# A hybrid encoder step on one core: a planner that lays out every instruction gets new rules for DMA issue, landing and stores

## The chip, the cores and the metric

The kernel runs on one core of one Trainium2 chip. The metric is device microseconds (us) of one execution; less is better. Three timed executions of the kernel before give a median of 1089.2 us (1089.12 to 1092.17).

## The reference

One inference step of an encoder layer, for 512 prompt tokens and 64 later tokens that are handled together (576 columns), in float32:

```python
x = x + mixer(rmsnorm(x))        # gated DeltaNet branch and gated linear attention branch, merged by gates, then w_o
x = x + cross_attn(rmsnorm(x), mem)   # 4 heads of 256 into 256 memory tokens: w_mk, w_mv, w_mq, w_mo
x = x + conv_ffn(rmsnorm(x))     # w_up (1024 -> 2*2816), causal depthwise conv, SiLU gate, w_down
y = rmsnorm(x)                   # and the new states, conv rows and memory keys/values as outputs
```

The model width is 1024, so `x` is eight tiles `x[0]` to `x[7]` of 128 features by 576 tokens. Nearly all work is matrix products of weights by those tiles.

## The kernel before

**Precision.** Each float32 product is made of float32r products: a weight tile is loaded raw (`wr`, 128 x 1024 float32, 512 KB), split into a high part `h` and a low part `lo` (both called `w`), and high x high, high x low and low x high are added in PSUM (`sm`). The split of most weights is "summed": ScalarE writes minus raw into `lo` and the rounded raw into `h`, and a second DMA from GpSimd's queue adds the weight from DRAM onto `lo` (`split_summed`, `accumulate`). The rest are split by a ScalarE copy and a subtraction on VectorE or GpSimd (`X`).

**Seven products for eight.** Many weights go in pairs of tiles through a scheme with seven half-size products, `P1`, `P2`, `P3`, `Q4` to `Q7`, in the order that `product_order` gives. `P1`, `P2` and `Q4` use a quarter of the raw weight pair, the others sums of quarters (`ws`, made on VectorE or GpSimd). In `products` each product is 4 x 3 matmuls; three banks hold the results (`a` for P1, Q6, Q7, Q4; `b` for Q5 and P3; `c` for P2), and `finish` adds a bank to the residual, after which the next product may write on it. For `w_o` this is `wo_finish`, a VectorE operation on `x[m]` or `x[m + 1]`, for the pairs of `WPAIRS` (0,1), (2,3), (4,5), (6,7).

**Stages around the change.** `ATT` sets the order after the mixer: memory keys and values (`mem_keys` with tile `kraw` and the store to `o_mk`; `mem_values` with `vraw` and `o_mv`), heads mk0, mv0, mv1, mk1, mk2, then the four `wo` pairs, then mv2, mk3, and the queries. The residual `x` is loaded a second time for `wo`, by `x_again`: all eight tiles at the first memory value (`("mv", 0)`). The last big stage is the FFN: `ffn_order` lays out the 22 up tiles (`upx` products from tile 4 on) and puts pieces of the down projection (`dn1`) behind up tiles by the table `AFTER`; what is left of them comes after the last up tile.

**What sets the order.** A planner, `Driver`, runs when the program is built. It keeps a clock `now` that follows TensorE, and a list of busy intervals for VectorE (`V`), ScalarE (`A`), GpSimd (`G`) and the transfer of the DMA rings (`D`). Every operation is placed in the first gap (`place`) that is not before its inputs and not more than `BACK` (6 us) before `now`; `put` hands its start to a heap, and `flush` emits the heap in order of those starts. So the planned times decide nothing but the order in which each engine's queue, and SyncE's DMA queue (SP), holds its instructions. On the chip each queue runs in that order and waits with semaphores. Raw weights live in five buffers (`RAWB` 4 and `RF` 1 in the later stages), split weights in nine (`WB` 6 and `WF` 3); `fetch` emits the loads of coming weights as soon as nine are enough for what is already split.

```python
def load(self, out, in_):
    cost = self.FIXED["D"] + free(out) * self.PACE["D"]          # 0.01 + columns * 0.0016
    start = self.place("D", max(self.ready_at(out), self.latest(self.seen, out)) + 2.2, cost)
    self.mark(self.wrote, start + cost, [out])
    self.put(start - 2.2, [(self.sync.dma_start, (out, in_), {})])
def store(self, out, in_, issuer=None):
    cost = self.FIXED["D"] + free(in_) * self.PACE["D"]
    start = self.place("D", self.ready_at(in_) + 2.2, cost)
    self.mark(self.seen, start + cost, [in_])
    self.put(start - 2.2, [((issuer or self.sync).dma_start, (out, in_), {})])
```

Of the kernel before, what the change touches and what calls it, by code (L numbers as in the profile page):

```python
# [14 lines left out]
ALU = mybir.AluOpType  # L15
# [3 lines left out]
D = 1024  # L19
# [18 lines left out]
HOP = 0.2  # L38
BACK = 6.0
MARGIN = 0.3  # L40
NWARM = 11


# [56 lines left out]
def product_order(pairs, late=False):  # L100

    seq = []
    for i, pair in enumerate(pairs):
        now = [(pair, p) for p in (("P1", "P2", "Q5", "Q6", "P3", "Q7") if late and i == 0 else
                                   ("P1", "Q5", "Q6", "P3", "Q7", "P2", "Q4") if i == len(pairs) - 1 else
                                   ("P1", "Q5", "Q6", "P2", "P3", "Q7"))]
        if i:
            now.insert(2, (pairs[i - 1], "Q4"))  # L110
        seq += now
    return seq
# [10 lines left out]
ATT = [("mk", 0), ("mv", 0), ("mv", 1), ("mk", 1), ("mk", 2), ("wo", 0), ("mv", 2), ("mk", 3), ("mq", 0), ("mq", 1), ("mq", 2), ("mq", 3), ("mv", 3)]  # L123
MPAIRS = [(("mo", m), ("mo", m + 1)) for m in range(2, 8, 2)]
JS = 4
AFTER = {7: 2, 8: 2, 9: 2, 10: 2, 13: 2, 14: 2, 15: 2, 16: 2, 20: 2, 21: 2}


def up_pair(j):
# [3 lines left out]
def ffn_order():  # L133

    seq, old = [("up", j) for j in range(JS)], []
    for j in range(JS, NJ):
# [3 lines left out]
        for i, q in ((j, "P1"), (j - 1, "Q7"), (j, "Q5"), (j, "P2"), (j - 1, "Q4"), (j, "Q6"), (j, "P3")):  # L140
            if i >= JS:
                seq.append(("upx", (i, q)))
        n = AFTER.get(j, 0)
        seq, old = seq + old[:n], old[n:]
# [36 lines left out]
def free(ap):  # L181
    n = 1
    for d in ap.shape[1:]:
        n *= d
    return n


class Engine:


    def __init__(self, drv, key, eng):
        self.drv, self.key, self.eng = drv, key, eng
# [4 lines left out]
    def weigh(self, calls):  # L197
        cost, aps, outs = 0.0, [], []
        for name, args, kw in calls:
# [5 lines left out]
            else:  # L205
                twice = self.key == "V" and len(ins) == 1 and self.port([(name, args, kw)])
                cost += self.drv.FIXED[self.key] + n * self.drv.PACE[self.key] * (0.5 if twice else 1.0)
            cost += 0.06 * (name == "scalar_tensor_tensor" or self.key == "V" and a[0].shape[-1] <= 128 and any(v.space == bass.MemoryType.PSUM for v in a[1:]))
# [41 lines left out]
class Driver:  # L250
# [1 line left out]

    FIXED = dict(V=0.15, A=0.17, G=0.2, D=0.01)
    PACE = dict(V=1 / 960, A=1 / 1180, G=1 / 465, D=512 / 320e3)

    def __init__(self, pe, sync):
        self.pe, self.sync = pe, sync
        self.chains = []  # L260
        self.done = set()
        self.now = 0.0
        self.half = self.type = None
        self.last = 0.0
        self.swapped = 0.0
        self.wrote = {}
        self.seen = {}
        self.ringed = {}
        self.busy = dict(V=[], A=[], G=[], D=[], port=[])
        self.ring = {}  # L270
        self.pending, self.fresh = set(), set()
        self.heap = []
        self.count = 0
        self.waiting = []
# [98 lines left out]
    def note(self, key, cost, outs, aps, fns, port=False):  # L373
# [4 lines left out]
        self.last = max(self.last, end)  # L378
        self.put(start, fns)

    def load(self, out, in_):
        cost = self.FIXED["D"] + free(out) * self.PACE["D"]
        start = self.place("D", max(self.ready_at(out), self.latest(self.seen, out)) + 2.2, cost)
        self.mark(self.wrote, start + cost, [out])
        self.put(start - 2.2, [(self.sync.dma_start, (out, in_), {})])

    def store(self, out, in_, issuer=None):
        cost = self.FIXED["D"] + free(in_) * self.PACE["D"]
        start = self.place("D", self.ready_at(in_) + 2.2, cost)
        self.mark(self.seen, start + cost, [in_])  # L390
        self.put(start - 2.2, [((issuer or self.sync).dma_start, (out, in_), {})])

    def accumulate(self, out, in_, issuer):

        issue = self.place("G", self.open([out], []), 1.0)
        cost = self.FIXED["D"] + 2 * free(out) * self.PACE["D"]
        end = self.place("D", issue + 2.0, cost) + cost + 1.0
        self.mark(self.wrote, end, [out])
        self.put(issue, [(issuer.dma_start, (out, in_), dict(accum_op=ALU.add))])

    def hold(self, fn, cost, args, kw):
        out, ins = args[0], args[1:]
# [38 lines left out]
    def advance(self, c):  # L441
        self.last = self.now
        r = next(c[1])
        if r is None:
            c[0] = self.last + MARGIN
        elif isinstance(r, list):
            c[0] = self.ready_at(*r) + MARGIN
        elif r != WAIT:
# [53 lines left out]
def tile_trunk(ctx, tc, xT, memT, wt, wd, vec, cst, w0, wgate, st_gdn, st_conv, st_gla, st_ffn, ckT, cv,  # L502
# [3 lines left out]
    V, A, G = Engine(drv, "V", nc.vector), Engine(drv, "A", nc.scalar), Engine(drv, "G", nc.gpsimd)  # L506
# [15 lines left out]
    def nm(s):  # L522
        cnt[0] += 1
        return f"{s}{cnt[0]}"

    def slot(s="s", dt=F32, w=SLOT):
        return drv.rotate("s", NS, sp.tile([P, w], dt, tag="s", name=nm(s)))
# [33 lines left out]
    def r4(ap, b=128):  # L561
        return ap.rearrange("p (a b) -> p a b", b=b)
# [180 lines left out]
    pw = pq.tile([P, 512], F32, tag="sm", name=nm("warm"))  # L743
    for _ in range(NWARM):
        PE.matmul(pw, ones_r, ones_r.unsqueeze(1).broadcast_to([P, 4, 128]), start=True, stop=True)
# [13 lines left out]
    for k in range(KT):  # L759
# [3 lines left out]
        if k in WPART:  # L763
            i, a, b = WPART[k]
# [136 lines left out]
    def use_norm(key):  # L901
        N["rt"], N["rbc"] = N[key]

    def xs_of(hl, w=T):
        return [(a[:, 0:w], b[:, 0:w]) for a, b in hl]
# [82 lines left out]
    def evac(ps, dst):  # L988
        for i, r, o in pieces(ps, N["rbc"], dst):
            V.tensor_tensor(o, i, r, op=ALU.mult)  # L990
# [691 lines left out]
    def xslot(i, s="x"):  # L1682

        return drv.rotate(f"F{i}", 1, fp.tile([P, SLOT], F32R if s != "x" else F32, tag=f"F{i}", name=nm(s), bufs=1))


    def main():
# [52 lines left out]
        for k in range(KT + 1):  # L1740
            for i, ps in enumerate(first2):
                j = k - i
# [210 lines left out]
        def x_again(m):  # L1953

            for i in (m, m + 1):
                x[i] = xslot(i)
                DMA(x[i][:, 0:T], xT[:, i, :])
# [4 lines left out]
        out = []  # L1962

        def wo_finish(pair, prod, a, b, c):
            m = pair[0][1]
            xx, scale = (x[m], 0.5) if prod in ("P1", "Q6", "P3", "P2") else (x[m + 1], -0.5)
            half = N1 if prod in ("P1", "P2", "Q4") else N2
            V.scalar_tensor_tensor(xx[:, half], b if prod in ("Q5", "P3") else c if prod == "P2" else a, scale, xx[:, half],
                                   op0=ALU.mult, op1=ALU.add)
            if prod == ("P2" if m == 6 else "P3"):  # L1970
                drv.spawn(c_norm(m, C_GMEM, acc, out))
            elif prod == "Q4":
                drv.spawn(c_norm(m + 1, C_GMEM, acc, out))

        def c_norm(m, gcol, acc_, out_):
            yield [x[m]]
            sq_acc(acc_, x[m], m == 0)
            drv.done.add(("sq", m))
            if drv.ready(*(("sq", i) for i in range(8))):
                drv.spawn(c_rstat("n2", [(acc_, 0)], 4, True, 2.0))  # L1980
            while not drv.ready("wo"):
                yield WAIT
            out_.append((m, norm_prep(x[m], vcol(gcol + m))))
            drv.done.add(("norm", gcol, m))

        for kd, i in ATT:
            if kd == "mk":
                yield from mem_keys(i)
            elif kd == "mv":
                if i == 0:  # L1990
                    for j in range(0, 8, 2):
                        x_again(j)
                yield from mem_values(i)
            elif kd == "wo":
                yield tuple(("wop1", m) for m in range(1, 8, 2))
                yield from products(WPAIRS, [wops[m] for m in range(1, 8, 2)], wo_finish, tuple(("wops", m) for m in range(1, 8, 2)))
                drv.done.add("wo")
            else:
                if i == 0:
                    yield tuple(("norm", C_GMEM, m) for m in range(8))  # L2000
                    xs = xs_of([p for _, p in sorted(out, key=lambda t: t[0])])
                ckr, cvr = slot("ckr"), slot("cvr")
                DMA(r4(ckr[:, 0:512], 256), ckT[:, 2 * i:2 * i + 2, :])
                DMA(r4(cvr[:, 0:512], 256), cv[:, 256 * i:256 * i + 256].rearrange("(a p) d -> p a d", p=P))
                N["ks", i], N["vs", i] = split(ckr), cvr
                for m in (2 * i, 2 * i + 1):
                    b = []
                    yield from tile_proj("mq", m, xs, b)
                    if m == 0:
                        yield ("n2",)  # L2010
                        use_norm("n2")
                    q = slot("q")
                    evac(b[0], q)
                    h, lo = slot("qh", F32R), slot("ql", F32R)
                    A.copy(h[:, 0:T], q[:, 0:T])
                    X.tensor_tensor(lo[:, 0:T], q[:, 0:T], f(h[:, 0:T]), op=ALU.subtract)
                    N["q", m] = (h, lo)
                drv.spawn(c_att(i))
# [239 lines left out]
        for kd, i in FFN[:-1]:  # L2258
            if kd == "up":
                j = i  # L2260
# [22 lines left out]
            elif kd == "dn1":  # L2283
                m, p = i
# [85 lines left out]
        late, early = [(256, TP, 0), (TP, T, 256)], [(0, 128, 0), (128, 256, 128)]  # L2370
# [213 lines left out]
```

## Time and profile before

| | before |
|---|---|
| median of three runs | 1089.2 us (1089.12 to 1092.17) |
| profiled execution | 1091.1 us, its span 1089.3 us |
| mean granted TensorE clock | 0.997 |
| DMA | 172.00 MB, mean 158 GB/s |
| TensorE busy | 1077.1 us of the span |

All instructions go through one line of the planner (L291), so tiles tell them apart and lines do not. PE is TensorE's matmuls, PEld its weight loads, DVE VectorE, ACT ScalarE, POOL GpSimd, SPq SyncE's DMA queue. A wait is put down to the operation that came last; an engine that is not the bottleneck may idle without cost.

### The profile page before, as it was taken

What the parts mean: (1) busy time and instruction counts of PE and PEld (TensorE: products, weight loads), DVE (VectorE), ACT (ScalarE), POOL (GpSimd) and SP (SyncE); (2) the same over time, 40 slices, a digit from 0 to 9 for tenths busy, and PEclk for the clock granted to TensorE, in tenths of its full rate; (3) what the DMA queues carried; (4) which work ended last, traced back from release to release, by engine and by line L of the source; (5) the groups of instructions that cost most, each with busy time, mean ns of one, the idle gap of its engine ahead of it and who ended that gap; (6) DMA issues with size and microseconds to landing.
All of it is one profiled execution on the core that took longest, in us unless ns stands there. A gap on an engine that the chain in (4) does not pass through costs nothing.

```text
span 1089.3 us, 21589 instructions
## 1 busy us (share of the span) xinstructions
PE 1077.1 (99%) x8278; PEld 1045.6 (96%) x8278; DVE 748.4 (69%) x1460; ACT 705.9 (65%) x1404; POOL 363.1 (33%) x578
## 2 busy tenths in 40 slices
PE   9999999999999999989999999999999999999997
PEld 8999989998988999989999999999999999999997
DVE  6666845776756676886835767767877776778565
ACT  6675546564747577465755668767876776677645
POOL 1243216133624333123410125444343333332224
PEclk9999999999999999999999999999999999999999
DMA  9666345253337889686685258777789688788834
GB/s 302 148 155 149 60 102 138 60 123 83 83 79 150 199 223 194 243 243 163 154 241 148 49 123 194 176 167 150 168 194 196 146 212 186 172 169 183 201 77 112
DMA packets 68040, 172.00 MB, mean 158 GB/s; under 512 B 7905, under 2 KB 14177, under 8 KB 67937
## 3 DMA queue, kind: packets, MB, share of 16 engines
q0 software_dynamic: 30672, 71.84, 38.4%
q1 hardware_dynamic: 36976, 98.26, 27.6%
q8 instruction: 65, 1.06, 0.4%
q10 hardware_dynamic: 288, 0.52, 0.1%
q14 instruction: 39, 0.31, 0.1%
HBM read 158.15 MB, written 5.37 MB: 150 GB/s over the span
## 4 chain that ended last, share of the span: by engine, by line
PE 95%; DVE 1%; DMA 1%; ACT 1%; issue 0%; SPq 0%; ACTq 0%; DVEq 0%
PE sm L291 95%; DMA wr<-wt 1%; DMA x<-xT 0%; DVE w L291 0%; DVE acl L291 0%; ACT w L291 0%; DVE ql L291 0%; DVE ws L291 0%; SPq L291 0%; ACT ach L291 0%; ACT ao L291 0%; ACT vraw L291 0%; DVE q L291 0%; DVE xl L291 0%; ACT xh L291 0%
## 5 line engine op out<-in xcount | busy, mean ns | idle before, releaser
L291 PE MATMUL sm<-xh,w 128*128 128x290 f32 (+3 forms) x2304 | 445.4, 300 | 0.5 <-ACT w L291 0.4
L291 PEld LDWEIGHTS sm<-xh,w 128*128 128x128 f32 x2304 | 356.0, 189 | 5.1 <-issue 1.7
L291 PE MATMUL sm<-xl,w 128*128 128x290 f32 (+3 forms) x1152 | 270.2, 296 | 0.3 <-DVE xl L291 0.2
L291 POOL DMA_DIRECT2D w<-wt x153 | 135.4, 898 | 373.8 <-ACT w L291 284.2
L291 PE MATMUL sm<-ach,w 128*128 128x256 f32 (+1 forms) x1216 | 232.3, 297 | 3.8 <-DVE x L291 3.4
L291 PEld LDWEIGHTS sm<-xl,w 128*128 128x128 f32 x1152 | 200.5, 188 | 0.8 <-DVE xl L291 0.8
L291 PEld LDWEIGHTS sm<-ach,w 128*128 128x128 f32 x1216 | 191.2, 189 | 4.6 <-ACT w L291 3.6
L291 ACT CAST w<-wr 128x512 fp32r<-128x512 f32 (+5 forms) x207 | 158.7, 769 | 19.6 <-PE sm L291 18.1
L291 ACT ACTIVATE w<-wr 128x512 fp32r<-128x512 f32 (+5 forms) x186 | 143.0, 770 | 22.3 <-PE sm L291 19.1
L291 PE MATMUL sm<-acl,w 128*128 128x256 f32 (+1 forms) x608 | 147.1, 296 | 0.3 <-DVE acl L291 0.3
L291 ACT CAST w<-ws 128x512 fp32r<-128x512 f32 (+1 forms) x132 | 78.5, 603 | 47.9 <-DVE ws L291 27.4
L291 PEld LDWEIGHTS sm<-acl,w 128*128 128x128 f32 x608 | 108.1, 189 | 0.5 <-DVE acl L291 0.5
L291 DVE TENSOR_TENSOR w<-ws,w 128x512 fp32r<-128x512 f32 (+1 forms) x104 | 75.2, 731 | 20.5 <-ACT w L291 18.3
L291 DVE SCALAR_TENSOR_TENSOR fc<-fu,vec,fc 128x578 f32<-128x578 f32 x88 | 70.5, 815 | 3.0 <-ACT fc L291 2.9
L291 PE MATMUL sm<-sh,w 128*128 128x290 f32 x288 | 61.2, 297 | 0.0
L291 DVE TENSOR_TENSOR x<-x,sm 128x320 f32<-128x320 f32 (+3 forms) x95 | 38.7, 436 | 30.8 <-PE sm L291 30.5
L291 POOL DMA_DIRECT2D w<-wd x33 | 29.0, 899 | 64.9 <-ACT w L291 58.0
L291 ACT ACTIVATE fc<-fu,vec 128x578 f32<-128x578 f32 x44 | 38.1, 871 | 16.9 <-POOL fu L291 16.4
L291 PEld LDWEIGHTS sm<-sh,w 128*128 128x128 f32 x288 | 47.6, 189 | 0.0
L291 PE MATMUL sm<-oh,w 128*128 128x256 f32 (+1 forms) x256 | 44.7, 295 | 0.0
L291 DVE TENSOR_TENSOR ws<-ws,wr 128x512 f32<-128x512 f32 (+1 forms) x64 | 42.9, 670 | 1.1
L291 POOL DMA_DIRECT2D w<-ws x27 | 23.6, 874 | 50.7 <-ACT w L291 50.2
(388 smaller groups left out, 1958.4 us busy)
## 6 DMA issues: line engine op xcount, KB each, us to landing
wr<-wt SPq DMA_DIRECT2D x130, 512.0 KB, 5.8
w<-wt POOLq DMA_DIRECT2D x52, 512.0 KB, 6.5
w<-wt POOLq DMA_DIRECT2D x101, 256.0 KB, 6.1
w<-ws POOLq DMA_DIRECT2D x27, 256.0 KB, 5.2
x<-xT SPq DMA_DIRECT2D x16, 288.0 KB, 5.9
wr<-wd SPq DMA_DIRECT2D x8, 448.0 KB, 5.3
w<-wd POOLq DMA_DIRECT2D x8, 448.0 KB, 7.1
wr<-wt SPq DMA_DIRECT2D x12, 256.0 KB, 4.7
```

Of the source, the lines that this page charges most:

```text
L291: fn(*args, **kw)
```

## The change

The planner's DMA rules are replaced, and four places in the order change:

```diff
+STORE = 1.0
+ISSUE, LATENCY, LANDING = 0.55, 2.0, 1.0
-        now = [(pair, p) for p in (("P1", "P2", "Q5", "Q6", "P3", "Q7") if late and i == 0 else
+        now = [(pair, p) for p in (("P1", "Q5", "P2", "Q6", "P3", "Q7") if late and i == 0 and pair[0][0] in ('wo',) else
+                                   ("P1", "P2", "Q5", "Q6", "P3", "Q7") if late and i == 0 else
-AFTER = {7: 2, 8: 2, 9: 2, 10: 2, 13: 2, 14: 2, 15: 2, 16: 2, 20: 2, 21: 2}
+AFTER = {7: 2, 8: 2, 9: 2, 10: 2, 13: 2, 14: 2, 15: 2, 16: 2, 21: 2}
-    FIXED = dict(V=0.15, A=0.17, G=0.2, D=0.01)
-    PACE = dict(V=1 / 960, A=1 / 1180, G=1 / 465, D=512 / 320e3)
+    FIXED = dict(V=0.15, A=0.17, G=0.2)
+    PACE = dict(V=1 / 960, A=1 / 1180, G=1 / 465, D=0.0014)
-        self.busy = dict(V=[], A=[], G=[], D=[], port=[])
+        self.busy = dict(V=[], A=[], G=[], D=[], S=[], port=[])
+    def moved(self, issued, ap, times=1.0):
+        cost = times * free(ap) * self.PACE["D"]
+        return self.place("D", issued + LATENCY, cost) + cost
     def load(self, out, in_):
+        at = self.place("S", max(self.ready_at(out), self.latest(self.seen, out)) + HOP, ISSUE)
+        self.mark(self.wrote, self.moved(at + ISSUE, out) + LANDING, [out])
+        self.put(at, [(self.sync.dma_start, (out, in_), {})])
     def store(self, out, in_, issuer=None):
+        at = self.place("S" if issuer is None else "A", self.ready_at(in_) + (HOP if in_.tensor.name.startswith("yo") else STORE), ISSUE)
+        self.mark(self.seen, self.moved(at + ISSUE, in_) + LANDING, [in_])
+        self.put(at, [((issuer or self.sync).dma_start, (out, in_), {})])
     def accumulate(self, out, in_, issuer):
-        issue = self.place("G", self.open([out], []), 1.0)
-        cost = self.FIXED["D"] + 2 * free(out) * self.PACE["D"]
-        end = self.place("D", issue + 2.0, cost) + cost + 1.0
+        at = self.place("G", self.open([out], []), 0.9)
+        self.mark(self.wrote, self.moved(at + 0.9, out, 1.2) + LANDING, [out])
         def wo_finish(pair, prod, a, b, c):
             m = pair[0][1]
+            if prod == "P1" and m < 4:
+                x_again(m + 4)
                 if i == 0:
-                    for j in range(0, 8, 2):
+                    for j in range(0, 4, 2):
                         x_again(j)
```

A load is issued, in the plan, when its buffer is free and SP has a gap of 0.55 us, whatever the rings carry; its data counts as landed after 0.55 + 2.0 us, the transfer and 1.0 us. A store is planned 1.0 us behind its data (0.2 us for the final output). `x[0]` to `x[3]` are loaded again where all eight were, `x[4]` and `x[5]` at the end of P1 of the first `wo` pair, `x[6]` and `x[7]` at that of the second. The first `wo` pair runs P1, Q5, P2, Q6, P3, Q7. Two `dn1` pieces move from behind up tile 20 to behind the last up tile. The sums that are computed stay the same.

## Rows read from the trace of the kernel before

**Rows 1.** The page's busy times: engine, us (share of span), number of instructions.
```profile
PE 1077.1 (99%) x8278; PEld 1045.6 (96%) x8278; DVE 748.4 (69%) x1460; ACT 705.9 (65%) x1404; POOL 363.1 (33%) x578
```

**Rows 2.** Waits of PE over the span: who for whom, total us, times, longest.
```profile
PE sm L291 <- DVE x L291: 3.4, 1, 3.4
...
PE sm L291 <- ACT ach L291: 0.5, 1, 0.5
```

**Rows 3.** Stretches: length, busy us (instructions) by engine, PE clock, DMA share, GB/s.
```profile
440.00:445.00 5.00, 5.00 (x40) 5.00 (x39) 5.00 (x8) 3.60 (x5) 3.17 (x1) 1.00 1.04 402
...
480.00:485.00 5.00, 5.00 (x40) 5.00 (x39) 3.12 (x7) 3.65 (x7) 1.87 (x3) 1.00 0.84 273
485.00:490.00 5.00, 1.64 (x11) 1.44 (x10) 4.87 (x8) 2.04 (x5) 2.46 (x2) 0.94 0.94 227
490.00:495.00 5.00, 5.00 (x30) 5.00 (x29) 2.52 (x5) 2.16 (x4) 0.88 (x1) 0.72 0.90 238
```

**Rows 4.** The chain that ended last, in 480 to 490: start, us, what.
```profile
475.42 5.85 DMA wr<-wt
...
481.89 1.13 ACT w L291 x2
...
486.48 1.53 DVE w L291
488.01 0.74 DVE x L291 x2
```

**Rows 5.** PE in order of time, 474 to 498: start, us, operation, idle before it.
```profile
479.00 1.76 PE L291 MATMUL sm<-hl,w 128*128 128x288 f32 x12
...
488.89 0.37 PE L291 MATMUL sm<-ach,w 128*128 128x288 f32 x1 [3.36 <-DVE x L291]
...
493.69 1.75 PE L291 MATMUL sm<-hl,w 128*128 128x288 f32 x12
```

**Rows 6.** SP's queue in order of time, 472 to 484: start, us, DMA issued.
```profile
474.98 0.39 SPq L291 DMA_DIRECT2D o_mk<-kraw  x1
475.42 1.42 SPq L291 DMA_DIRECT2D wr<-wt  x2
...
481.57 0.82 SPq L291 DMA_DIRECT2D wr<-wt  x2
```

**Rows 7.** Waits of SP's queue, 440 to 500: for whom, total us, times, longest.
```profile
SPq L291 <- DVE kraw L291: 9.2, 2, 5.3
SPq L291 <- ACT vraw L291: 8.3, 2, 4.6
```

**Rows 8.** DVE in order of time, 466 to 500: the last readers of raw buffers.
```profile
465.84 1.22 DVE L291 TENSOR_TENSOR w<-wr,w 128x1024 fp32r<-128x1024 f32 x1
...
470.30 2.36 DVE L291 TENSOR_TENSOR w<-wr,w 128x1024 fp32r<-128x1024 f32 x2 [0.26 <-ACT w L291]
```

**Rows 9.** DMA issues, us to landing: span; at 472.1; at 482.3; 425 to 500.
```profile
wr<-wt SPq DMA_DIRECT2D x130, 512.0 KB, 5.8
...
w<-wt POOLq DMA_DIRECT2D x1, 256.0 KB, 4.1
...
w<-wt POOLq DMA_DIRECT2D x1, 256.0 KB, 7.8
...
x<-xT SPq DMA_DIRECT2D x8, 288.0 KB, 7.9
```

**Rows 10.** SP's queue, 300 to 470: the second load of x.
```profile
432.65 10.87 SPq L291 DMA_DIRECT2D x<-xT  x8
```

**Rows 11.** The page's DMA queues: packets, MB, share of 16 engines over the span.
```profile
q0 software_dynamic: 30672, 71.84, 38.4%
q1 hardware_dynamic: 36976, 98.26, 27.6%
```

**Rows 12.** A stretch of the FFN, and the chain's last long piece.
```profile
975.00:1000.00 25.00, 25.00 (x189) 25.00 (x188) 22.06 (x38) 21.85 (x38) 9.65 (x23) 1.00 0.92 208
...
849.08 234.32 PE sm L291 x1764
```

More of the change, by code (lines that the diff above doesn't have):

```diff
@@ L379, in note @@
         self.put(start, fns)
+    def moved(self, issued, ap, times=1.0):
+        cost = times * free(ap) * self.PACE["D"]
+        return self.place("D", issued + LATENCY, cost) + cost
     def load(self, out, in_):
[L382 to L385, printed above, removed]
+        at = self.place("S", max(self.ready_at(out), self.latest(self.seen, out)) + HOP, ISSUE)
+        self.mark(self.wrote, self.moved(at + ISSUE, out) + LANDING, [out])
+        self.put(at, [(self.sync.dma_start, (out, in_), {})])
     def store(self, out, in_, issuer=None):
[L388 to L391, printed above, removed]
+        at = self.place("S" if issuer is None else "A", self.ready_at(in_) + (HOP if in_.tensor.name.startswith("yo") else STORE), ISSUE)
+        self.mark(self.seen, self.moved(at + ISSUE, in_) + LANDING, [in_])
+        self.put(at, [((issuer or self.sync).dma_start, (out, in_), {})])
     def accumulate(self, out, in_, issuer):
-        issue = self.place("G", self.open([out], []), 1.0)
-        cost = self.FIXED["D"] + 2 * free(out) * self.PACE["D"]
-        end = self.place("D", issue + 2.0, cost) + cost + 1.0
-        self.mark(self.wrote, end, [out])
-        self.put(issue, [(issuer.dma_start, (out, in_), dict(accum_op=ALU.add))])
+        at = self.place("G", self.open([out], []), 0.9)
+        self.mark(self.wrote, self.moved(at + 0.9, out, 1.2) + LANDING, [out])
+        self.put(at, [(issuer.dma_start, (out, in_), dict(accum_op=ALU.add))])
     def hold(self, fn, cost, args, kw):
```

## The prediction

> **What bounds the kernel now.** I read the busy times first: PE works 1077.1 us of a span of 1089.3 [rows 1], and no other engine is above 69%. So the change can't make work shorter: it moves no matmul out of the program, and all it can win is time in which PE stands still or runs at its lower clock. That is little, so the second view is the list of PE's waits [rows 2]. One wait of 3.4 us stands out, for VectorE's `x`; the next largest is 0.5 us. The third view is the table of stretches, to see what the wait costs in all [rows 3]. In five microseconds PE does 40 matmuls in the stretch 480 to 485, but 11 in 485 to 490 and 30 in 490 to 495: 29 + 10 = 39 are missing, and at 5.00/40 = 0.125 us each that is 4.9 us. 3.36 us of it are the standstill itself [rows 5]; the other 1.5 come from the granted clock, which reads 0.94 and then 0.72 after the standstill [rows 3]: a mean between the full level (2.4 GHz) and half of it (1.2 GHz). So the prize is 4.9 us, 0.45% of the time, in one place, and the fourth view, the chain there, has to say why [rows 4].
>
> The place is the first `wo` pair. PE starts P1 at 479.00 and stands still from 488.89 - 3.36 = 485.5 [rows 5], so P1, P2, Q5 and Q6 take 1.6 us each; P3 starts at 488.89, as its bank `b` is still to be read by `wo_finish`. Read backwards [rows 4]: those reads (DVE `x`, 488.01) stand in VectorE's queue behind weight splits (DVE `w`, 486.48), these behind ScalarE's casts (481.89), and ScalarE had stopped for the landing of a raw weight, issued at 475.42 and landed 5.85 us later. By order of use that weight is tile 2, of the **second** pair. So PE stands still for a bank of pair 1 since two in-order queues were held up by a load for pair 2 that came later than the plan had thought.
>
> Why it came late is in SP's queue [rows 6, 7]. The two loads of the second pair are issued at 475.42 right behind the store of `kraw`, and SP had stood at that store: its longest wait for `kraw` is 5.3 us. The buffers were free before that: VectorE's last reads of the two raw tiles ended at 465.84 + 1.22 = 467.1 and about 470.30 + 1.2 = 471.5 [rows 8]. So the loads lost up to 8.3 and about 4 us, the first partly since the planner emits no load more than 6 us ahead of its clock. The stores of `vraw` hold SP up in the same way twice, up to 4.6 us [rows 7].
>
> **The change part by part.** *Stores behind their data; SP as an engine.* Two things move the loads ahead of the store. The store is planned 1.0 us later, and a load no longer waits in the plan for a gap in the transfers. A load that goes out when its buffer and the 6 us limit allow it goes at about 470 to 471.5 rather than at 475.42 to 476.4, so I take 4 us earlier; the bounds are 0 (the order stays) and 5.4 (475.42 less 470). It costs the store some microseconds, and nobody waits for it: the next writer of that slot is one of 57 tiles away. Where a store is passed by loads whose buffer isn't free, SP stands at the load and the store behind it waits; that too costs nothing on PE.
>
> *Loads that land later.* The old plan had a 512 KB load landed 2.2 + 0.01 + 1024 x 0.0016 = 3.85 us after its issue, the new one 0.55 + 2.0 + 1024 x 0.0014 + 1.0 = 4.98; the trace has a median of 5.8 over 130 loads [rows 9]. ScalarE's split of tile 2 is thus planned about 1.1 us later against the issue, behind casts of the first pair that need no DMA. That takes away the second half of the mechanism: ScalarE's idle while the first pair's splits are waiting. The remaining error is 5.8 - 4.98 = 0.8 us per load, and more where rings are full.
>
> *Accumulates.* A 256 KB one was planned to land 2.0 + 1.65 + 1.0 = 4.65 us after its issue, and is now at 0.9 + 2.0 + 0.86 + 1.0 = 4.76. The trace has 4.1 in a quiet moment and 7.8 at 482.3 [rows 9], so the plan is too early in both cases; this is an unpaid cost, taken up below.
>
> *P1, Q5, P2.* Nothing is added. Q5 is pulled ahead by one product, 1.6 us, and the accumulate of P2 gets 1.6 us more. I cost it at nothing: Q5's weight is a sum that VectorE makes without a second DMA. If its operands weren't ready it would cost up to 1.6 us.
>
> *x in halves.* Four of eight loads of 288 KB leave the stretch at 432 to 443 [rows 10], in which the rings are full (1.04) with PE unhindered [rows 3]: no gain there. Two of them come at P1 of the first pair, at most 6 us ahead of the planner's clock, so near 475 to 481. They are used two pairs later, 22 us on, against 7.9 us to land [rows 9]: no wait for themselves. What they may cost others is 2 x 0.295 MB over 273 to 402 GB/s [rows 3], 1.5 to 2.2 us of transfer ahead of or beside the second pair's weights.
>
> *dn1 pieces.* Two pieces behind the last up tile instead of behind tile 20. PE has no idle time from 849 to 1083 [rows 12], at up to 0.92 DMA share, so there is nothing to win; I cost it at nothing, as up tiles without such pieces between them (17 to 19, for instance) already lie in that piece.
>
> **What is late next.** Without the standstill P1 of the second pair is due at 479.00 + 6 x 1.6 = 488.6 instead of 493.69 [rows 5]. Its low part is accumulated by the DMA at 482.3 that took 7.8 us [rows 9]: landed at 490.1, 1.5 us too late. So taking away the ScalarE stop alone would win only about 4.9 - 1.5 = 3.4 us; the rest has to come from the loads going out earlier. With 4 us earlier loads and up to 2.2 us lost to `x`, the low part is there at 488.3 or before, just in time. I allow 0.4 us for what is left over.
>
> **The sum.** -4.9 + 0.4 = -4.5 us. The profiled execution took 1091.1 us, 1.8 beyond its span and 1.9 above the median of the runs; a difference carries over, so the span goes to 1084.8 and the median from 1089.2 to **1084.7**.
>
> **The rivals.** *A: the next wait takes over.* The loads stay late (0 us earlier) and the `x` halves fall in front of them. P1 of the second pair then stands for 1.5 + 1.5 to 2.2 = 3.0 to 3.7 us, and with the clock's 1.5 up to 5.2. The time is 1089.2 - 4.9 + 3.0 to 5.2 = 1087.3 to 1089.5. For it speaks the 7.8 us landing and the 0.84 to 0.94 DMA share there [rows 3, 9]; against it the buffers that are free early [rows 8]. The Trainium skill, "DMA: Bandwidth & Descriptors", section "Queues, rings and completion order", speaks for A: each DMA engine takes a ring's descriptors in order and takes turns between rings, so `x` tiles that SP issues ahead of weights go first. No row here shows such an `x` load at the `wo` pairs; the halves come there only with the change.
>
> *B: it doesn't do what it says here.* The planned times shift, but store and loads keep their order, and the splits too: 1089.2.
>
> *C: slower.* The new plan charges an accumulate 1.2 times a load's transfer. The queues say otherwise: 38.4% for 71.84 MB against 27.6% for 98.26 MB [rows 11], 0.534 against 0.281% per MB, a ratio of 1.9. Where accumulates fill the rings, in the FFN at 0.92 [rows 12], the old plan charged 1.65 us for each 256 KB one and so pushed loads apart; the new one charges 0.86 and lets them go at once, with splits planned for a landing that comes too early. If a landing there is later than planned by more than the lead of ScalarE's and VectorE's queues on PE, the stop of [rows 4] is repeated. One is worth 4.9 us, and two, with the old one gone, give 1089.2 - 4.9 + 9.8 = 1094.1. For it: 18 up pairs offer the chance, and the order of all instructions is new. Against it: the old plan had its landings too early as well, and PE never stood there.
>
> **How the numbers follow.** Forecast 0.52, A 0.22, B 0.06, C 0.20. About 0.3% (3.3 us) is what a measurement of this kernel can tell from no change. The forecast lies beyond that, A and B within: faster 0.52, same 0.28, slower 0.20. The forecast's own range is 1083.3 (the whole prize, and the 0.5 us wait and as much again) to 1085.9. For 8 in 10 it takes in A and B and stops within C: 1082.9 to 1093.5, about a twentieth left out below and a tenth above.
>
> **What would show it.** Right: PE's wait for `x` near 485 gone or below 1 us, 40 matmuls in each five microseconds from 480 to 500, and clock 1.00 there; in SP's queue two weight loads ahead of the `kraw` store. A shows as a PE wait for a weight at the second pair's P1 near 488, behind a POOL accumulate; B as the same wait in the same place; C as PE idle in 650 to 1080, with ScalarE waiting for a raw weight's landing. I am wrong altogether if PE's instructions or their busy time change by more than 1 us, as the order of its small float32 matmuls between the big ones is also new.

## The result, and the profile after

The changed kernel takes 1096.35 us (median of 6 runs, 1095.05 to 1097.92) where the kernel before took 1090.02 beside it: a ratio of 1.0048 [1.0036, 1.0061] by the record, some 5.2 us slower (the two medians lie 6.3 us apart). The forecast was 1084.7, the range ended at 1093.5. The profiled execution took 1096.05 us with a span of 1094.3, 5.0 more than before.

The busy times of the changed kernel, to be held against [rows 1]:

```profile
PE 1079.1 (99%) x8278; PEld 1046.6 (96%) x8278; DVE 758.5 (69%) x1464; ACT 703.2 (64%) x1404; POOL 361.0 (33%) x574
```

PE has the same 8278 matmuls and is 2.0 us longer at them; the other 3 us by which the span grew are standstills. PE's waits after the change, as in [rows 2] (for whom, total us, times, longest):

```profile
PE sm L294 <- DMA w<-wt: 2.3, 1, 2.3
PE sm L294 <- DVE x L294: 1.1, 1, 1.1
PE sm L294 <- DVE S L294: 1.1, 1, 1.1
PE sm L294 <- ACT gt L294: 1.1, 2, 0.7
PE warm L294 <- POOL onesr L294: 1.0, 1, 1.0
PE sm L294 <- DVE gt L294: 0.9, 1, 0.9
PE sm L294 <- DMA w<-ws: 0.6, 1, 0.6
```

The wait for `x` has fallen from 3.4 to 1.1 us; the forecast wanted it gone or below 1. Instead there are a new one of 2.3 us for an accumulated weight, and four small ones for `S` and `gt`. The stretches at the `wo` pairs and at 700 say what the clock adds (length, busy us and instructions of PE, PEld, DVE, ACT, POOL, then PE clock, DMA share, GB/s); the last line is the kernel before:

```profile
485.00:490.00 5.00, 4.77 (x37) 4.54 (x35) 4.81 (x7) 3.04 (x7) 2.84 (x3) 1.00 1.07 307
490.00:495.00 5.00, 4.08 (x31) 4.11 (x32) 4.39 (x10) 2.94 (x5) 0.88 (x1) 1.00 1.06 339
...
700.00:725.00 25.00, 24.32 (x167) 23.69 (x168) 14.97 (x25) 16.43 (x23) 10.06 (x20) 0.93 0.90 196
```

```profile
700.00:725.00 25.00, 25.00 (x184) 24.59 (x183) 16.27 (x27) 18.72 (x27) 11.10 (x24) 1.00 0.80 179
```

At the `wo` pairs PE now does 37 and 31 matmuls in the two stretches in which it did 11 and 30 [rows 3], at clock 1.00. At 700 it is the other way round: 167 in 25 us at clock 0.93, where the kernel before did 184 at 1.00. 25 x 0.07 = 1.75 us of that stretch are clock. That doesn't explain the 2.0 us by which PE's busy time grew, as the kernel before lost nearly as much to the clock behind its own standstill: divided at the landmarks below, busy time grew by 1.5 us in the mixer, fell by 1.3 at the `wo` pairs, and grew by 0.7 and 1.1 in the two parts behind them.

A balance by landmarks, the start of a kind of matmul on PE before (L291) and after (L294):

```profile
L291 PE MATMUL sm<-mh,w x128: 277/281/388, 450.6 to 541.3; 128*128 128x256 f32 x128
L294 PE MATMUL sm<-mh,w x128: 274/280/384, 454.8 to 541.8; 128*128 128x256 f32 x128
...
L291 PE MATMUL sm<-hl,w x120: 289/294/397, 328.4 to 517.4; 128*128 128x288 f32 x120
L294 PE MATMUL sm<-hl,w x120: 290/294/300, 333.0 to 518.1; 128*128 128x288 f32 x120
```

The mixer, up to the first matmul of the memory keys (`mh`): 450.6 and 454.8, **+4.2**. From there to the last `hl` of the `wo` pairs: 66.8 and 63.3, **-3.5**. From there to the first matmul on `sh`, an operand of the paired up products: 219.2 and 221.1, **+1.9**. From there to the output transposes: 340.0 and 341.8, **+1.8**. The rest is +0.6, the sum +5.0. So there was a gain at the `wo` pairs, and the other parts of the kernel gave back more than it.

**The `wo` pairs.** SP's queue there, to be held against [rows 6], and PE's P1 and P3 of the first pair, against [rows 5]:

```profile
473.45 2.69 SPq L294 DMA_DIRECT2D wr<-wt  x2
476.20 2.16 SPq L294 DMA_DIRECT2D x<-xT  x2
478.46 5.84 SPq L294 DMA_DIRECT2D o_mk<-kraw  x2
```

```profile
483.25 1.75 PE L294 MATMUL sm<-hl,w 128*128 128x288 f32 x12
...
490.92 0.37 PE L294 MATMUL sm<-ach,w 128*128 128x288 f32 x1 [1.14 <-DVE x L294]
```

The second pair's raw weights are issued ahead of the `kraw` stores. The first of them goes 9.8 us ahead of P1 (483.25 - 473.45), where it was 3.6 (479.00 - 475.42): 6.2 us earlier, more than the 4 forecast and than their upper bound of 5.4. SP now stands 5.8 us in the two stores, and nobody waits for that.

**The place at 700.** PE, and the queue of GpSimd ahead of it (start, us, operation, idle before and its releaser), and third the DMA issues there (KB each, median us to landing):

```profile
700.68 0.81 PE L294 MATMUL sm<-xh,w 128*128 128x290 f32 x4 [2.25 <-DMA w<-wt]
```

```profile
688.53 4.11 POOL L294 TENSOR_TENSOR rt<-rin,mhalf 128x5 f32<-128x5 f32 x1 [4.32 <-DVE rin L294]
692.61 2.69 POOL L294 DMA_DIRECT2D w<-wt  x3
```

```profile
w<-wt POOLq DMA_DIRECT2D x3, 512.0 KB, 11.8
```

The kernel before, in the same place:

```profile
687.35 0.88 POOL L291 DMA_DIRECT2D w<-wt  x1 [1.88 <-ACT w L291]
...
689.86 3.37 POOL L291 TENSOR_TENSOR rt<-rin,mhalf 128x5 f32<-128x5 f32 x1 [1.48 <-DVE rin L291]
693.19 1.81 POOL L291 DMA_DIRECT2D w<-wt  x2
```

`rt` is the power of the reciprocal root of the norm, five columns. Before, one accumulate of 512 KB goes out ahead of it, at 687.35, and lands 5.2 us later. After, `rt` stands ahead of all three: GpSimd waits 4.32 us for `rin`, works 4.11 us, and only then issues them, together. The first is on the chain of waits from 692.61 for 8.03 us, to 700.64, and PE goes on at 700.68.

The plan charges that power 0.3 + 5 x 0.165 = 1.1 us. By itself it takes little more: the same power of the norm before it, on the same shape, took 1.20 us.

```profile
540.93 1.20 POOL L294 TENSOR_TENSOR rt<-rin,mhalf 128x5 f32<-128x5 f32 x1 [0.18 <-DVE rin L294]
```

What differs is VectorE. Beside this one it was busy for 0.03 us, beside the one at 688.53 for 3.05 of 4.11 us:

```profile
688.53:692.64 4.11, 4.11 (x33) 4.11 (x33) 3.05 (x7) 4.11 (x6) 4.11 (x2) 1.00 0.51 138
```

Those seven VectorE steps have two operands each in SBUF, and the power ends about 1.1 us behind the last of them. That they hold it up is argued from these rows; no run takes them away. The stop has a second half too: the plan has the accumulate landed 5.6 us after its issue, which from 692.61 is 698.2, just before PE ran out of work (700.68 - 2.25 = 698.43), but it took 8.03.

**The mixer.** Four stops, none of them behind a DMA. The first, PE, then VectorE and GpSimd in the same microseconds:

```profile
165.46 0.49 PE L294 MATMUL sm<-S,c 128*128 128x128 f32 x2 [1.11 <-DVE S L294]
```

```profile
161.48 3.66 DVE L294 SCALAR_TENSOR_TENSOR z<-zt,z 128x576 f32<-128x576 f32 x1
165.07 0.33 DVE L294 SCALAR_TENSOR_TENSOR S<-S,dl,sm 128x128 f32<-128x128 f32 x1
```

```profile
161.04 1.38 POOL L294 TENSOR_TENSOR tg<-cst,ggh 128x512 fp32r<-128x512 f32 x1
162.06 1.36 POOL L294 TENSOR_TENSOR tg<-cst,ggl 128x512 fp32r<-128x512 f32 x1
163.07 1.45 POOL L294 TENSOR_TENSOR e<-gc 128x576 f32<-128x576 f32 x1
```

`S` stands behind a `z` that takes 3.66 us; of the eight `z` of this form the median is 759 ns. The last stop, at 424, is ScalarE's queue: a copy out of PSUM stands behind two casts of a weight and a `gt` step, and PE goes on at 424.48, when it is through:

```profile
420.99 1.06 ACT L294 ACTIVATE w<-wr 128x1024 fp32r<-128x1024 f32 x1 [0.63 <-ACT gt L294]
...
424.05 0.37 ACT L294 COPY gt<-sm 128x288 f32<-128x288 f32 x1
```

The four stops are 1.1 + 0.9 + 0.7 + 0.4 = 3.1 us, but some small idle time of the kernel before is gone: up to the landmark PE is idle for 4.6 us where it was 1.9. So 2.7 of the 4.2 us are standstill, and 1.5 are longer busy time for the same 3558 matmuls, at a granted clock that reads 1.00 in every stretch of 5 us. What makes them longer wasn't looked for.

### The profile page after: what moved, and what is told of

It reads as the page before. It is cut to its first block, busy times and chain, and to the rows that moved or that the text cites. A ratio compares the mean times of both kernels' runs of the same rounds, so it can differ in the third digit from the quotient of the medians.

```text
span 1094.3 us, 21597 instructions
## 1 busy us (share of the span) xinstructions
PE 1079.1 (99%) x8278; PEld 1046.6 (96%) x8278; DVE 758.5 (69%) x1464; ACT 703.2 (64%) x1404; POOL 361.0 (33%) x574
## 4 chain that ended last, share of the span: by engine, by line
PE 92%; DMA 3%; DVE 2%; ACT 2%; issue 1%; POOL 0%; SPq 0%; ACTq 0%; POOLq 0%; DVEq 0%
PE sm L294 92%; DMA w<-ws 2%; DMA w<-wt 1%; ACT w L294 1%; DVE tu L294 0%; DVE z L294 0%; DMA wr<-wt 0%; DVE w L294 0%; ACT gt L294 0%; DVE x L294 0%; ACT cx L294 0%; ACT xh L294 0%; DVE xl L294 0%; DVE ws L294 0%; DVE on L294 0%
## 5 line engine op out<-in xcount | busy, mean ns | idle before, releaser
L294 PE MATMUL sm<-xh,w 128*128 128x290 f32 (+3 forms) x2304 | 448.8, 300 | 2.5 <-DMA w<-wt 2.3
L294 PEld LDWEIGHTS sm<-xh,w 128*128 128x128 f32 x2304 | 358.0, 189 | 7.1 <-DMA w<-wt 2.5
L294 PE MATMUL sm<-xl,w 128*128 128x290 f32 (+3 forms) x1152 | 270.3, 296 | 0.2 <-DVE xl L294 0.2
L294 POOL DMA_DIRECT2D w<-wt x153 | 136.5, 901 | 333.6 <-ACT w L294 265.1
L294 PE MATMUL sm<-ach,w 128*128 128x256 f32 (+1 forms) x1216 | 231.0, 296 | 2.2 <-DVE x L294 1.1
L294 PEld LDWEIGHTS sm<-xl,w 128*128 128x128 f32 x1152 | 200.6, 189 | 0.7 <-DVE xl L294 0.7
L294 PEld LDWEIGHTS sm<-ach,w 128*128 128x128 f32 x1216 | 189.8, 188 | 3.7 <-ACT gt L294 1.5
L294 ACT CAST w<-wr 128x512 fp32r<-128x512 f32 (+5 forms) x207 | 158.7, 769 | 4.0 <-PE sm L294 3.6
L294 ACT ACTIVATE w<-wr 128x512 fp32r<-128x512 f32 (+5 forms) x186 | 143.3, 770 | 20.6 <-PE sm L294 17.4
L294 PE MATMUL sm<-acl,w 128*128 128x256 f32 (+1 forms) x608 | 146.4, 295 | 0.0
L294 ACT CAST w<-ws 128x512 fp32r<-128x512 f32 (+1 forms) x132 | 78.5, 604 | 49.7 <-DVE ws L294 27.4
L294 PEld LDWEIGHTS sm<-acl,w 128*128 128x128 f32 x608 | 107.5, 188 | 0.0
L294 DVE TENSOR_TENSOR w<-ws,w 128x512 fp32r<-128x512 f32 (+1 forms) x103 | 71.7, 707 | 23.6 <-ACT w L294 21.7
L294 DVE SCALAR_TENSOR_TENSOR fc<-fu,vec,fc 128x578 f32<-128x578 f32 x88 | 70.5, 815 | 3.0 <-ACT fc L294 2.9
L294 PE MATMUL sm<-sh,w 128*128 128x290 f32 x288 | 61.6, 298 | 0.7 <-DMA w<-ws 0.6
L294 DVE TENSOR_TENSOR x<-x,sm 128x320 f32<-128x320 f32 (+3 forms) x95 | 38.6, 436 | 31.3 <-PE sm L294 31.0
L294 POOL DMA_DIRECT2D w<-wd x33 | 28.6, 885 | 83.6 <-ACT w L294 81.4
L294 PEld LDWEIGHTS sm<-sh,w 128*128 128x128 f32 x288 | 47.5, 189 | 1.3 <-DMA w<-ws 1.2
L294 ACT ACTIVATE fc<-fu,vec 128x578 f32<-128x578 f32 x44 | 38.2, 870 | 15.4 <-POOL fu L294 15.3
L294 PE MATMUL sm<-oh,w 128*128 128x256 f32 (+1 forms) x256 | 44.6, 295 | 0.0
L294 DVE TENSOR_TENSOR ws<-ws,wr 128x512 f32<-128x512 f32 (+1 forms) x63 | 43.4, 689 | 1.0
L294 POOL DMA_DIRECT2D w<-ws x27 | 23.4, 867 | 50.4 <-ACT w L294 38.1
```

The source lines that it names most:

```text
L294: fn(*args, **kw)
```

## The experiments

The theory after the result: the change itself does at the `wo` pairs most of what was forecast, and loses its gain because every planned time moves, and with it the order of every engine's queue, ScalarE's from 17 us on and VectorE's from 49. The rivals: (1) the order changes (`x` in halves, P1-Q5-P2, `dn1`) do harm; (2) the new price of an accumulate does harm, as rival C had it; (3) the slowdown is a property of the new DMA rules as such.

**The two halves of the change.** The order changes alone, with the old rules:

```diff
-        now = [(pair, p) for p in (("P1", "P2", "Q5", "Q6", "P3", "Q7") if late and i == 0 else
+        now = [(pair, p) for p in (("P1", "Q5", "P2", "Q6", "P3", "Q7") if late and i == 0 and pair[0][0] in ('wo',) else
+                                   ("P1", "P2", "Q5", "Q6", "P3", "Q7") if late and i == 0 else
...
-AFTER = {7: 2, 8: 2, 9: 2, 10: 2, 13: 2, 14: 2, 15: 2, 16: 2, 20: 2, 21: 2}
+AFTER = {7: 2, 8: 2, 9: 2, 10: 2, 13: 2, 14: 2, 15: 2, 16: 2, 21: 2}
...
+            if prod == "P1" and m < 4:
+                x_again(m + 4)
...
-                    for j in range(0, 8, 2):
+                    for j in range(0, 4, 2):
```

> The kernel before with the four changes of the order alone (first w_o pair P1, Q5, P2; x loaded again in halves; two dn1 pieces behind the last up tile) and the old DMA rules. Its order up to the first w_o pair is that of the kernel before. Theory 'rules' (the new DMA rules bring the new stops, the changes of the order are worth nothing): 1090 us, within 1.5 of the kernel before, PE's wait for x of 3.4 us at 485 still there. Theory 'changes of the order' (they bring the win at the w_o pairs): 1086 us or less, that wait gone. Theory 'shuffle' (any new order has stops of its own): anywhere from 1086 to 1097.

Measured: 1092.55 beside 1092.12, ratio 0.9999 [0.9989, 1.0010]. The wait for `x` stays, 2.9 us. Rival 1 is out, and the zero that the prediction put on these edits is right within that interval.

The rules alone, with these four places undone in the changed kernel:

> The changed kernel without the four changes of the order: the new DMA rules alone. Its order up to the first w_o pair is that of the changed kernel. Theory 'rules': 1096 us, within 1.5 of the changed kernel; the stops of 0.6 to 1.3 us at 165, 306, 352 and 424 are there (they must be, the order is the same), the wait for x near 490 is at most 1.2 us, and PE stands near 700 behind an accumulate. Theory 'changes of the order': the wait for x stays at 3 us or more, and the time is above 1098.

Measured: 1097.32, 1.0039 [1.0023, 1.0055]. The mixer has the same stops as the changed kernel, the wait for the accumulate behind `rt` is 3.9 us, and the one for `x` 1.5. The whole effect comes from the rules.

**Which of the rules.** The new accumulate price alone, in the kernel before:

```diff
-        issue = self.place("G", self.open([out], []), 1.0)
-        cost = self.FIXED["D"] + 2 * free(out) * self.PACE["D"]
+        issue = self.place("G", self.open([out], []), 0.9)
+        cost = 1.2 * free(out) * 0.0014
```

> The kernel before with the new accumulate rule alone (0.9 us to issue, 1.2 times a load's transfer at 0.0014 us per column). Theory 'accumulates' (charged too little, they are what makes the plan wrong; the rival that the prediction priced): 1094 us or more, with PE waits behind accumulates in the FFN. Theory 'loads' (the new rule of loads moves the splits): within 1.5 us of the kernel before, the wait for x at 485 still there at 3 us or so.

Measured: 1095.32 beside 1091.51, 1.0035 [1.0024, 1.0047]. PE's longest waits:

```profile
PE sm L291 <- ACT gt L291: 2.6, 1, 2.6
PE sm L291 <- DVE x L291: 2.5, 2, 1.3
PE sm L291 <- DMA w<-wt: 1.4, 3, 0.8
PE sm L291 <- DVE xi L291: 1.1, 1, 1.1
```

It is slower, but not where rival C had it: PE has no stop at all from 725 to 1060, where the accumulates are densest. The longest, 2.6 us, is at 385 behind ScalarE's copy of `gt` in the mixer; others are behind VectorE's queue at 156, 347, 494 and 1073. Three, 1.4 us in all, are for accumulated weights, at 487, 489 and 704.

The reverse, all new rules but the old accumulate price, without the order changes:

```diff
-        at = self.place("G", self.open([out], []), 0.9)
-        self.mark(self.wrote, self.moved(at + 0.9, out, 1.2) + LANDING, [out])
+        at = self.place("G", self.open([out], []), 1.0)
+        cost = 0.01 + 2 * free(out) * 512 / 320e3
+        self.mark(self.wrote, self.place("D", at + 2.0, cost) + cost + 1.0, [out])
```

> The new rules of loads and stores with the old accumulate rule, without the four changes of the order. Theory 'accumulates': 1088 us or less, the win at the w_o pairs without new stops. Theory 'loads': the stops in the mixer (165, 306, 352, 424) and near 700 stay, 1095 to 1097.

Measured: 1097.61, 1.0055 [1.0037, 1.0072]. Taking the suspected price away doesn't help: the four stops of the mixer go, the one at 700 shrinks to 0.9 us, and others come, near 235 and 370 in the mixer and at 860 (1.0) and 981 (2.3) in the FFN, the last two for accumulated sums (`w<-ws`). So the new price is enough for a slowdown, but not needed for one: rival 2 is out as the only cause.

Stores planned 1.0 us behind their data, alone, in the kernel before:

```diff
-        start = self.place("D", self.ready_at(in_) + 2.2, cost)
+        start = self.place("D", self.ready_at(in_) + (0.0 if in_.tensor.name.startswith("yo") else 1.0) + 2.2, cost)
```

> The kernel before with the stores planned 1.0 us behind their data and nothing else. SyncE's order differs in two places, the others' behind the middle of the program alone. If the win at the w_o pairs comes from loads that pass the stores: the wait for x falls from 3.4 us to 1.2 or less and the time is 1086 us. If it comes from splits that are planned for later landings: the wait stays at 3 us or more, 1090.

Measured: 1091.26, 0.9998 [0.9987, 1.0010]. This run doesn't test what it was made for. SP's order differs near 320 us and from 525 to 543, and not at the `wo` pairs: the loads of the second pair still stand behind the store of `kraw`, 3.4 us ahead of P1 (479.5).

```profile
475.60 0.39 SPq L291 DMA_DIRECT2D o_mk<-kraw  x1
476.05 1.50 SPq L291 DMA_DIRECT2D wr<-wt  x2
```

The two waits that PE has at the `wo` pairs and behind them:

```profile
487.99 0.37 PE L291 MATMUL sm<-ach,w 128*128 128x288 f32 x1 [1.92 <-DVE x L291]
523.24 0.37 PE L291 MATMUL sm<-ach,w 128*128 128x288 f32 x1 [1.36 <-DVE x L291]
```

The old wait falls from 3.36 to 1.92 us without a load that passes a store; ScalarE's and VectorE's orders differ there from 480 us on. 35 us later a second wait takes its place, and the sum is the same. The store rule alone wins nothing, and doesn't put the loads ahead of the store.

**How much a reordering costs by itself.** Four nudges that change one planned constant by about one to five per cent. Three in the kernel before: the time between engines, 0.20 to 0.21 us; the planner's margin; ScalarE's fixed cost:

```diff
-HOP = 0.2
+HOP = 0.21
```

> The kernel before with one constant of the planner moved by 0.01 us (HOP, the time from one engine to the next, 0.20 to 0.21). No rule and no step is changed, but hundreds of places in every engine's order move. Theory 'rules': within 1.5 us of the kernel before, as nothing in it knows the DMA better or worse. Theory 'shuffle': 3 us or more away, most likely slower, with stops at other places than the kernel before.

```diff
-MARGIN = 0.3
+MARGIN = 0.31
```

> The kernel before with MARGIN 0.31 us instead of 0.30 and the old DMA rules: hundreds of places move, nothing in it knows the DMA better. Theory 'rules': within 1.5 us of the kernel before. Theory 'shuffle': 2 to 6 us slower, with stops at places of its own, in the mixer too.

```diff
-    FIXED = dict(V=0.15, A=0.17, G=0.2, D=0.01)
+    FIXED = dict(V=0.15, A=0.172, G=0.2, D=0.01)
```

> The kernel before with ScalarE's planned fixed cost 0.172 us instead of 0.170 and the old DMA rules. Theory 'rules': within 1.5 us of the kernel before. Theory 'shuffle': 2 to 6 us slower, with stops at places of its own.

Measured: 1.0016 [1.0007, 1.0026], 1.0011 [1.0002, 1.0020] and 1.0048 [1.0032, 1.0064]. None is faster, and the last is as slow as the change under study. The theory 'shuffle' did not get all that it asked for: it wanted 3 us or more from the first and 2 to 6 from the second, and they gave 1.7 and 1.2, the second within the 1.5 us of the other theory. The waits of the last:

```profile
PE sm L291 <- DVE x L291: 3.9, 1, 3.9
PE sm L291 <- DVE xi L291: 1.5, 1, 1.5
PE sm L291 <- DVE vg L291: 1.5, 1, 1.5
PE sm L291 <- DMA w<-ws: 1.2, 1, 1.2
```

2 ns on each planned ScalarE instruction say nothing true or false about a DMA, and they cost PE three new stops of 1.2 to 1.5 us. So the order before was one with few stops, and a new order can have stops of its own. Against a spread of 0.1 to 0.5% from nudges, the 0.48% of the change doesn't show that the new rules are worse: rival 3 isn't refuted, but it is not needed, and it is not shown either.

One nudge in the changed kernel:

```diff
-ISSUE, LATENCY, LANDING = 0.55, 2.0, 1.0
+ISSUE, LATENCY, LANDING = 0.55, 2.02, 1.0
```

> The changed kernel with the planned DMA latency 2.02 us instead of 2.00. TensorE's and SyncE's orders stay word for word; VectorE, ScalarE and GpSimd differ in the FFN alone. Theory 'rules': within 1 us of the changed kernel. Theory 'shuffle': the stop at 700 (order unchanged there) stays, but those of 0.3 to 0.9 us at 811 and 979 move or go, and others come: 1 to 3 us either way.

Measured: 1097.04, 1.0043 [1.0028, 1.0059]. PE's and SP's orders are the same as without it, and so are the stops in the mixer. The one at 700 is in the same place, but takes 3.9 us instead of 2.3: there the first accumulate behind `rt` landed after 9.7 us instead of 8.0.

**The place at 700, by itself.** In the changed kernel the planner is told that `rin` is ready 1.2 us later, for this one norm, so that the accumulate goes ahead of `rt`:

```diff
+        if key == "n3":
+            drv.mark(drv.wrote, drv.ready_at(rin[:, 0:k]) + 1.2, [rin[:, 0:k]])
```

> The changed kernel with one thing different: in the third norm (c_rstat with key n3) the planner takes rin as written 1.2 us later, so that the first of the three 512 KB accumulates stands ahead of the power operation (rt) in GpSimd's queue instead of behind it. SyncE's and ScalarE's orders stay word for word, VectorE's differs in 4 rows, GpSimd's in 8. Theory 'GpSimd's queue' (the stop at 700 is the accumulate that stands behind rt, which itself waits for rin): the wait of 2.3 us and the lower clock behind it go, 1092.3 us. Theory 'full rings' (the accumulate lands late as the DMA rings are full): the wait stays at 2 us or more, 1096.

Measured: 1091.14 beside 1091.51, 0.9992 [0.9983, 1.0002]. GpSimd's queue is now that of before:

```profile
688.62 0.88 POOL L294 DMA_DIRECT2D w<-wt  x1 [4.35 <-ACT w L294]
689.23 3.54 POOL L294 TENSOR_TENSOR rt<-rin,mhalf 128x5 f32<-128x5 f32 x1
692.74 1.80 POOL L294 DMA_DIRECT2D w<-wt  x2
```

The wait for the accumulate is gone, the mixer's stops are as they were. From the last `hl` to the first matmul on `sh` it takes 217.0 us instead of 221.1: 4.1 us, about the 2.25 of standstill and 1.75 of clock. Some twenty-five instructions of GpSimd, VectorE and PE that stand in another order are worth 0.56% against the changed kernel (1.0048 to 0.9992). That settles that the order of GpSimd's queue is the cause at 700: the accumulate itself took 7.2 us to land here, but was issued 4 us earlier. How long PE stands when all three go out behind `rt` depends on their landing and on when PE needs them; in the six kernels with that order it is 0.4 (r_acc) to 3.9 us.

**The mixer, by itself.** The changed kernel, with the old DMA rules until the memory keys and values are planned, where `new` is set, and the new ones from there on. The load is shown; the store and the accumulate have the same branch with their old rules:

```diff
+    new = False
...
     def load(self, out, in_):
+        if not self.new:
+            cost = 0.01 + free(out) * 512 / 320e3
+            start = self.place("D", max(self.ready_at(out), self.latest(self.seen, out)) + 2.2, cost)
+            self.mark(self.wrote, start + cost, [out])
+            self.put(start - 2.2, [(self.sync.dma_start, (out, in_), {})])
+            return
...
+        drv.new = True
```

> The changed kernel in which the old DMA rules hold until the memory keys and values begin (all of the mixer is planned as before) and the new ones from there on; the four changes of the order are in. ScalarE's and SyncE's orders in the mixer are those of the kernel before. Both theories: the mixer's stops at 165, 306, 352 and 424 are gone, the wait for x at the w_o pairs is 1.2 us or less, and the stop near 696 behind rt stays (2 to 4 us and the lower clock). 1092 us, 3 to 4 less than the changed kernel.

Measured: 1091.16 beside 1091.70, 0.9995 [0.9985, 1.0005]. The memory keys start at 450.7 us, as before, without the four stops; the `wo` pairs keep their gain (63.3 us to the last `hl`). What is left is `rt` again:

```profile
698.00 1.34 PE L295 MATMUL sm<-xh,w 128*128 128x290 f32 x4 [3.74 <-DMA w<-wt]
```

Both together, late rules and the 1.2 us for `rin`:

> The same with rin of the third norm taken as written 1.2 us later in the plan, so that one accumulate stands ahead of rt. If the three places are independent and add up: 1091.1 of the changed kernel with that step alone, less 3.3 for the mixer: 1087 to 1088 us, and below the kernel before by 3 us. If the lost time comes back somewhere else: 1090 or more.

Measured: **1086.54** (1086.21 to 1088.72) beside 1091.70, 0.9957 [0.9944, 0.9970]. This is faster than both kernels. Its span is 1084.4 us, and all of PE's waits are:

```profile
PE sm L295 <- DVE x L295: 1.1, 1, 1.1
PE warm L295 <- POOL onesr L295: 1.0, 1, 1.0
PE sm L295 <- DMA w<-ws: 0.6, 1, 0.6
PE sm L295 <- DVE xl L295: 0.2, 1, 0.2
```

With the mixer as before and the queue at 700 as before, what remains of the change is a gain of 1091.70 x 0.0043 = 4.7 us, where 4.5 were forecast. That the two agree is luck. By the spans it is 4.9: 3.5 at the `wo` pairs (66.8 to 63.3 us), one less than forecast; another 2.1 between there and the first matmul on `sh` (219.2 to 217.1), where the kernel before has three small stops (0.29 at 621, 0.47 and 0.26 at 645) that are gone and that the prediction left out; and 0.7 lost in the other parts.

## Why the prediction was wrong, point by point

- **What bounds the kernel; the cause of the wait.** The bound is right, the cause only in part shown. The loads go 6.2 us earlier relative to P1, the wait is 1.1 instead of 3.4 us, and the clock stays at 1.00. In all seven kernels with the new load and store rules at this place the loads go 9.5 to 9.9 us ahead of P1, and the wait is 0.9 to 1.5. Where they stand behind the store (3.4 to 4.5 us ahead of P1) it is 2.9 to 3.9 in five kernels, but 1.9 in r_store and 1.2 in r_acc: the orders of ScalarE and VectorE can shorten it with the loads as late as ever. No run moves the loads alone. (The next largest wait of the kernel before is not 0.5 us but 1.0, for `onesr` at the start; it is the same after.) The gain of that place was put at 4.5 us and is 3.5, as the wait didn't vanish: the DVE `x` that PE waits for starts at 490.32, when two splits of weights (487.99, 2.41 us) ahead of it are done. The 0.4 us allowed for a rest was too small by 1.0.
- **The edits costed at nothing.** Right: P1-Q5-P2, `x` in halves and the `dn1` pieces together are 0.9999.
- **The store.** Right for its own cost. The prediction named two things that move the loads, the later store and a load that doesn't wait for a gap in the transfers; r_store shows that the first alone doesn't move them. What the second alone does wasn't tried.
- **Rival A.** The `x` halves went out at 476.20, behind the second pair's weights and not ahead of them, so its condition didn't come about. The order of a ring was not put to a test.
- **The step that failed: the sum.** It had one term, the place where the kernel before stood still, and took the rest of the program as it was. But a planner that is given other times for DMAs decides anew between any two instructions whose times are close, on all engines. The parts of the kernel without a wait in [rows 2] were not parts where nothing could be lost; they were parts where this one order had come out well. What the runs showed in its place: +4.2 us in the mixer, 4.0 at 700 and 1.8 in the FFN, against 3.5 won at the `wo` pairs and 2.1 won between them and 700, which nobody had forecast. The nudges of the kernel before show what the step should have carried: +0.1 to +0.5% (1 to 5 us) for a new order, with no sign of a gain in three tries.
- **Rival C.** Right in its sign and nearly in its size (1094.1), wrong in place and for the most part in mechanism. It looked for landings later than planned in the dense accumulates of the FFN; r_acc has no stop there and r_oldacc, with the old price, has two. A landing later than planned (8.0 us instead of 5.6) is half of the stop at 700, though, and 0.6 us of the FFN's loss is a wait for one at 979.7. Its argument against itself, that PE never stood there before, was the same mistake as in the sum. The larger stops are an in-order queue that waits ahead of DMA issues (700: 4.0 us of time), and VectorE's and ScalarE's queues in the mixer (4.2 us), where no DMA ends the wait.
- **The range.** Its upper end lay just within rival C, which had two stops of 4.9 us; there were five new ones in the mixer and at 700, 8 us in all, beside small losses in the FFN. The clock was sized well: the standstill of 2.25 us at 700 cost 1.75 more, where the prediction had 1.5 for one of 3.36.
- **The tests named.** "Two weight loads ahead of the `kraw` store" and clock 1.00 came true, the wait is 1.1 instead of below 1. PE did not do 40 matmuls in each five microseconds: 43, 37, 31 and 40 from 480 to 500. PE's busy time changed by 2.0 us, more than the 1 named as the sign that the prediction is wrong altogether, and the sign holds: the clock lost at 700 replaces about as much lost at 490 before, and the largest growth, 1.5 us, is in the mixer, where the small matmuls are. Whether their order makes it wasn't looked for. C's sign, PE idle in 650 to 1080, came at 698 and 979, but for accumulates and not with ScalarE waiting for a raw weight.

What stays open: which comparison of planned times moves each of the four stops into the mixer wasn't traced, only that the DMA rules in force during the mixer do (late_rules). And of the +1.8 us in the FFN, 0.8 are gone in fix_rt (341.8 to 341.0) and 0.6 are the wait at 979.7; the rest wasn't looked for.

## What to carry to other kernels

A new cost in a planner that orders a whole kernel is two changes: the effect that it is meant for, and a reshuffle of everything else, which is to be priced by nudges that mean nothing before a gain or a loss is put down to the rule. Let the new rule hold only from the stretch that has the wait, and then read the waits again: here the rule from the memory keys on gave 0.9995, and with the one queue at 700 put right 0.9957, where the rule for the whole program had 1.0048. In an in-order queue that issues DMAs, look for the slow or waiting instruction ahead of the issues: a power over five columns, planned 3 us too short for that place, cost 4.0 us, nearly as much as the whole change was to win.

## What the runs showed of the hardware

- GpSimd's power of 128x5 took 1.20 us at 27.12 and at 540.93 in the changed kernel, with VectorE nearly idle beside it, and 3.36 to 4.11 us at the third norm in all fourteen traces, where VectorE runs two-operand steps back to back. So it isn't the power that is slow. The cause wasn't tested by a run.
- The VectorE `z` with two operands in SBUF took 3.66 us while GpSimd ran three two-operand steps (161.04 to 164.5), against a median of 0.76. Another took 2.33 beside a GpSimd step of 1.74 us (233.52) that began before it, and one 0.78 though a GpSimd step began 0.07 us behind it (273.43). The Trainium skill, "SBUF — State Buffer", section "Who interferes with whom", says that a VectorE instruction with two SBUF inputs contends with a GpSimd instruction that reads SBUF; the first two rows agree, the third doesn't show it. The cause wasn't tested by a run; the kernel before has one such `z` as well, 3.05 us, which cost PE nothing.
- Three accumulates of 512 KB issued together at 692.6 took 11.8 us in the median to land, one ahead of the power 5.2 in the kernel before (687.35) and 7.2 in fix_rt (688.62). The plan has 0.9 + 2.0 + 1.72 + 1.0 = 5.6 for each, and queues only their transfers.
